# Two transformer blocks on one core: three pairs of heads kept, and a pair's solve issued later

## The chip, the cores and the metric

One core of a Trainium2 chip runs the whole program. The metric is device time in microseconds (us) of one execution; the median of three runs of the kernel before is 2461.56 us (2458.64 to 2461.78). The engines are called TensorE (PE; PEld is its weight load), VectorE (DVE), ScalarE (ACT), GpSimd (POOL) and SyncE (SP), as the profile names them.

## The reference, cut to what matters

Two blocks work on 256 tokens with 2048 channels, all in float32. The first has a gated delta rule over 16 heads of 128 channels, a convolution branch with a layer norm, gates and an output product; the second has latent attention and another convolution branch. The part that the change touches computes, for each head, in chunks (the kernel takes chunks of 128 tokens, the reference 64):

```
A = einsum(kb, k) * decay * strict            # kb = k * beta
T = triangular_solve(eye + A, eye)            # unit lower triangular inverse
u = T @ (v * beta);  w = T @ (kb * exp(gc))
v_new = u - w @ S;  o = q_dec @ S + qk @ v_new;  S = S * exp(g_last) + k_end^T @ v_new
```

and, for the convolution branch, `layernorm(u) = (u - mean) * rsqrt(mean((u - mean)^2) + eps) * g + b` over the 2048 channels of a token.

## The kernel before

Channels lie on the partitions and the 256 tokens on the free axis. Every weight matrix streams through the core as 128x512 tiles (SyncE loads them, 512 KB in one DMA). ScalarE makes a rounded copy `hi` of each (line 231), VectorE the rest `lo` (line 234), and TensorE forms each product from three matmuls (`mm3`, lines 256 to 258). `hi` and `lo` are made three to four tiles ahead of their use.

The order of all work is written out by hand: every engine executes its instructions in the order in which the program issues them. The main stream issues one `mm3` after the other; after each one `tick` (line 191) counts one tick, and then steps the background chains that are due. A chain is a generator: `yield n` puts its next step n ticks later. So a chain's delays set only where its instructions stand between those of the main stream on each engine's queue; if their data are not ready there, the engine stands still, with everything that is queued behind. `force` steps the earliest chain ahead of its time.

In the head stage each head takes 64 ticks (`group`: 16 k-tiles of four output tiles). After it the chain `evac` (line 573) convolves q, k and v into the tile `qkv`; 30 ticks after the second head of a pair has ended, the chain `delta` (line 592) of that pair begins. At most two deltas are active, so with 128 ticks for a pair the end of one overlaps with the start of the next. `head` waits at line 568 until the output of the pair that used the same `qkv` tile is done (two tiles: `heads < h - 2`). After the eight pairs come the four groups of `ga` (256 ticks; `L824` evacuates them with a sigmoid, the first at tick 64 after the last head), and later `z_b`, beside which the layer norm's chain runs.

The steps of `delta` and `output`, in ticks after the delta's first step (k, q and v of the next pair begin 128 ticks later):

```
  0  L607 eight transposes to t1 (TensorE); L614 four squares (ScalarE)
  2  L618 four squares, L619 two copies (ScalarE)
  7  L621 (VectorE), L623 pow (GpSimd)
 11  L629 to L634 coefficients (VectorE); L640 eight products (TensorE)
 15  L646 nt, 18 L646 pt (VectorE)
 20  L660 transposes, L662 (ScalarE), L668;  21 L672 (VectorE)
 25  L676 DMA dd<-dg (issued by ScalarE);  33 L678 DMA bl<-dd (ScalarE), L680 (GpSimd)
 42  L684, L686: 15 columns, two GpSimd instructions each
 84  L694 tt (VectorE)
 88  L702 transposes (TensorE), L703 copy to ta (ScalarE);  92 product, z;  96 product, L715
100  L702, L703;  104 L724;  108 L731;  112 L702, L703 copy to tt
116  L740 products, L741 copy to z;  120 L745 products, L746 copy
124  values(0): L752, L754, L759;  128 L763, L765 copy to st;  131 L769, L770, L772, L776
135  values(1);  139 L708, L781, L782
143  L793 squares;  148 L797, L799 pow (GpSimd);  152 L802;  159 L806 transposes, L808;  163 L811
```

All these chains take their PSUM banks in turn from four (`pss`). The layer norm (line 868) subtracts the mean from eight pairs of channel tiles, squares each on ScalarE and adds the squares on GpSimd (`pool_square`, seven ticks a pair); then it waits six ticks (line 888) and `rms` adds the two halves (line 324), sums over the partitions (line 330), takes the power on GpSimd (line 335) and spreads it (line 339).

Of the kernel before, what the change touches and what calls it, by code (L numbers as in the profile page):

```python
# [18 lines left out]
T = 256  # L19
# [28 lines left out]
def _mats():  # L48
# [5 lines left out]
    def put(name, v):  # L54
# [23 lines left out]
AHEAD = 3  # L78
RM = (3, 6)
WARM = 10  # L80
Y = dict(silu=8, ssq=5, pow=4, coef=2, gram=4, diag=4, dma1=8, dma2=9, rec=3, wait=21, base=4, copy=4, pred=4, vn=4, st=3, vs=4, on=3, so=5,
         f=4, scale=7)
PN = 4
RATES = (0.31, 0.10, 0.37)
# [23 lines left out]
class Build:  # L108
# [52 lines left out]
        self.idle(WARM)  # L161

    def idle(self, n):
        """Products on constants that keep the array's clock up while it waits for data."""
        if n:
            q = self.ps()
        for _ in range(n):
            self.nc.tensor.matmul(q[:, :P], self.ones, self.ones, start=True, stop=True, skip_group_check=True)
# [2 lines left out]
        self.nc.scalar.copy(hi, src)  # L171
        self.nc.vector.tensor_tensor(out=lo, in0=src, in1=hi.bitcast(F32), op=ALU.subtract)

# [1 line left out]
    def chain(self, gen, delay=0, limited=False):  # L175
        (self.waiting if limited else self.active).append([self.now + delay, gen, limited])

# [31 lines left out]
            self.step(min(self.active, key=lambda c: c[0]))  # L209
            self.admit(True)  # L210

# [1 line left out]
    def fetch(self, upto):  # L213
        while self.loaded <= min(upto, self.nhalf - 1):
            raw = self.rawp.tile([P, 2, 512], F32, tag="raw", name="raw")
# [43 lines left out]
        self.tick()  # L259

    def group(self, xs, nk=NT, done=None):
        """Four output tiles; with done, they end one after the other, and done(pb, ct) follows each."""
        pb = self.banks()

        def unit(ws, k, ct):
            s = slice(ct * P, ct * P + P)
            x = xs[ct] if isinstance(xs, list) else xs
            while x.ready <= k:
                self.force()
            self.mm3(pb[ct // 2][:, ct % 2], (ws[0][:, s], ws[1][:, s]), (x.hi[:, k], x.lo[:, k]),  # L270
                     k == 0 and ct % 2 == 0, k == nk - 1)

        for k in range(nk - 4 if done else nk):
            ws = self.kt()
            for ct in range(4):
                unit(ws, k, ct)
        if done:
            ws = self.quad()
            for n, ct in enumerate((0, 2, 1, 3)):
                for k in range(4):  # L280
                    unit(ws[k], nk - 4 + k, ct)
                done(pb, ct, n)
        return pb
# [4 lines left out]
        self.tick()  # L288

    def rows(self, xs):  # L290
        """512 outputs with the tokens on the partitions, one bank for each half of the tokens."""
        pb = self.banks()
        for k in range(NT):
            ws = self.kt()
            while xs.ready <= k:
                self.force()
            for c in range(2):
                self.unit(pb, c, xs, k, ws)
        return pb
# [7 lines left out]
            self.mm3(pb[:, 0], (hi[:, s], lo[:, s]), (xs.hi[:, k], xs.lo[:, k]), k == 0, k == NT - 1)  # L307
        return pb

# [1 line left out]
    def square_into(self, acc, src, first):  # L311
        nc = self.nc
        n = src.shape[1]
# [41 lines left out]
        return Operand(self.big(t1, F32R, name=name + "h"), self.big(t2, F32R, name=name + "l"), ready)  # L355

    def split_chain(self, make, src, x, ks, gap):
        """make(k) emits src(k); the two parts of x follow one and two steps behind."""
        nc = self.nc
        n = len(ks)  # L360
        for j in range(n + 2):
            if j < n:
                make(ks[j])
            if 1 <= j <= n:
                k = ks[j - 1]
                nc.scalar.copy(x.hi[:, k], src(k))
            if j >= 2:
                k = ks[j - 2]
                nc.vector.tensor_tensor(out=x.lo[:, k], in0=src(k), in1=x.hi[:, k].bitcast(F32), op=ALU.subtract)  # L369
                x.ready = (k.stop if isinstance(k, slice) else k + 1)  # L370
            yield gap(j)
# [4 lines left out]
        return t  # L376

    def scaled(self, src, gname, x, gap, hook):
        """x = src * g in two parts, which follow hook(k) at once and one step behind."""
        nc = self.nc  # L380
        for j in range(NT + 1):
            if j < NT:
                hook(j)
                nc.scalar.activation(x.hi[:, j], src[:, j], AF.Copy, scale=self.vec(gname, j))
            for k in ([0] if j == 0 else [j - 1] if j > 1 else []):
                nc.vector.scalar_tensor_tensor(out=x.lo[:, k], in0=src[:, k], scalar=self.vec(gname, k),
                                               in1=x.hi[:, k].bitcast(F32), op0=ALU.mult, op1=ALU.subtract)
                x.ready = k + 1
            yield gap(j)
# [39 lines left out]
            next(gen)  # L429
        self.chain(gen, delay)  # L430

# [1 line left out]
    def glu(self, j, xs, scaled=False):  # L433
        nc = self.nc
        pb = self.group(xs)
# [126 lines left out]
    def head(self, wk, h):  # L562
        nc = self.nc
        tl = lambda name, shape, **k: wk.tile([P] + shape, F32, tag=name, name=name, **k)
        pb = self.group(self.h)
        a = h % 2
        if a == 0:
            while self.heads < h - 2:
                self.force()
            self.pair = (tl("qkv", [2, 3, T], bufs=2), tl("zs", [2, T], bufs=3))  # L570
        qkv, zs = self.pair

        def evac():
            src = (pb[0][:, 0], pb[0][:, 1], pb[1][:, 0])
            w = lambda i, j: self.vec("w_qkv", (i * H + h) * 4 + j)
            for i in range(3):
                nc.scalar.activation(qkv[:, a, i], src[i], AF.Copy, scale=w(i, 3))
            nc.scalar.activation(zs[:, a], pb[1][:, 1], AF.Silu)
            yield 2
            for s in range(1, 4):  # L580
                for i in range(3):
                    nc.vector.scalar_tensor_tensor(out=qkv[:, a, i, s:], in0=src[i][:, :T - s], scalar=w(i, 3 - s),
                                                   in1=qkv[:, a, i, s:], op0=ALU.mult, op1=ALU.add)
                    yield 2
            nc.scalar.activation(qkv[:, a], qkv[:, a], AF.Silu)
            yield Y["silu"]
            if a:
                self.chain(self.delta(wk, h - 1, qkv, zs), 0, True)

        self.chain(evac())  # L590

    def delta(self, wk, h, qkv, zs):
        """Two heads, h and h + 1; four chunks f = 2 a + c of 128 tokens."""
        nc = self.nc
        mm = nc.tensor.matmul
        kw = dict(start=True, stop=True, skip_group_check=True)
        tl = lambda name, shape, **k: wk.tile([P] + shape, F32, tag=name, name=name, **k)
        half = lambda c: slice(c * P, c * P + P)
        ident = self.mat("ident")
        AC = [(a, c) for a in range(2) for c in range(2)]  # L600
        four = lambda t: t.rearrange("p (f t) -> p f t", f=4)
# [14 lines left out]
        for a in range(2):  # L616
            for j in (0, 1):
# [6 lines left out]
                                op=ALU.pow)  # L624
        yield Y["pow"]
        nk, nb = tl("nk", [2, 2]), tl("nb", [2, 2])
# [8 lines left out]
        vs = qkv[:, :, 2].rearrange("p a (c t) -> p a c t", c=2)  # L635
        gr = []
        for a in range(2):
            g = self.ps()
# [22 lines left out]
        for a, c in AC:  # L661
            nc.scalar.activation(vs[:, a, c], t2[:, half(2 * a + c)], AF.Copy, scale=nk[:, a, c:c + 1])  # L662

        # inverses of the diagonal blocks of 16, one column after the other
        b16 = self.blk[:, 0:P]
        bl = tl("bl", [16, 4, 16])
        flat = bl.rearrange("p l c i -> p (l c i)")
# [25 lines left out]
        z, vn = tl("z", [4, P]), tl("vn", [2, 2, P])  # L693
# [70 lines left out]
        st = tl("st", [2, P])  # L764
# [9 lines left out]
        on = nt.rearrange("p (a c) t -> p a c t", a=2)  # L774
# [93 lines left out]
    def layernorm(self):  # L868
        nc = self.nc
        cv = self.cv  # L870
        acc = self.new_acc()
        nc.gpsimd.tensor_tensor(out=acc, in0=cv[:, 0:2], in1=cv[:, 2:4], op=ALU.add)
        for c in range(2, 8):
            nc.gpsimd.tensor_tensor(out=acc, in0=acc, in1=cv[:, 2 * c:2 * c + 2], op=ALU.add)
        yield 32
        q = self.ps()
        for a in range(2):
            nc.tensor.matmul(q[:, :T], self.ones, acc[:, a], start=(a == 0), stop=(a == 1))
        mb = self.nrm.tile([P, T], F32, tag="rb", name="rb", bufs=3)
        nc.scalar.activation(mb, q[:, :T], AF.Copy, scale=1.0 / D)  # L880
        yield 4
        sq = self.new_acc()
        for c in range(8):
            s = slice(2 * c, 2 * c + 2)
            nc.vector.tensor_tensor(out=cv[:, s], in0=cv[:, s], in1=self.bc(mb, 2), op=ALU.subtract)
            self.pool_square(sq, cv[:, s], c == 0)
            yield 7
        yield 6
        got = []
        yield from self.rms(sq, D, got)  # L890
        yield 3
        for c in range(8):
            s = slice(2 * c, 2 * c + 2)
            nc.vector.tensor_tensor(out=cv[:, s], in0=cv[:, s], in1=self.bc(got[0][1], 2), op=ALU.mult)
            yield 3
            for k in (2 * c, 2 * c + 1):
                nc.scalar.activation(cv[:, k], cv[:, k], AF.Silu, scale=self.vec("ln_g", k), bias=self.vec("ln_b", k))
# [502 lines left out]
        self.final(mx, x)  # L1400

    def final(self, xs, x):
        """w_out_2 with tokens on the partitions; x goes there by the array's transposes."""
        nc = self.nc
        wk = self.ctx.enter_context(self.tc.tile_pool(name="fin", bufs=1))
        g = wk.tile([P, D], F32, name="g_row")
# [41 lines left out]
        for j in range(3):  # L1448
            pb = self.rows(xs)
# [3 lines left out]
        pb = self.banks()  # L1453
# [119 lines left out]
```

## Time and profile before

| what | value |
|---|---|
| median of three runs | 2461.56 us |
| span of the profiled execution (the page shows no time of its own beside it) | 2464.7 us |
| TensorE busy | 2399.9 us (97%) |
| TensorE weight loads busy | 2279.6 us (92%) |
| VectorE busy | 1655.2 us (67%) |
| ScalarE busy | 1321.8 us (54%) |
| GpSimd busy | 182.1 us (7%) |
| weights read by SyncE's queue | 417.99 MB |
| head stage | about 255 to 735 us of the span |
| layer norm's sum of squares | about 990 to 1020 us |

The profile is of one execution. Times are counted from the start of the span. A line such as `L702` names the source line that issued the instruction; `s` is a PSUM bank of the background chains, `pb` one of the main stream. The granted clock is a share of TensorE's full 2.4 GHz: 1.00, or 0.50 for its lower level, 1.2 GHz. All DMAs are issued by SyncE and ScalarE.

### The profile page before, as it was taken

To read this page: it belongs to the slowest core of one execution; us is meant where nothing else is said; L and a number is where in the kernel's file an instruction comes from. 1 tells how busy PE (TensorE), PEld (TensorE's weight loads), DVE (VectorE), ACT (ScalarE), POOL (GpSimd) and SP (SyncE) were. 2 spreads that over 40 slices of the span, in tenths; PEclk is the share of its full clock that TensorE was granted. 3 is DMA by queue.
4 is the path that set the end of the run, shared out by engine and by line. 5 is a ranking of instruction groups with operands and counts; after the bars stand their busy time and mean duration, and the time that the engine had idled before them with its cause. 6 is when DMAs were issued, how large, how long until landed. Compare 5 with 4: busy or idle time off the path is not lost.

```text
span 2464.7 us, 47419 instructions
## 1 busy us (share of the span) xinstructions
PE 2399.9 (97%) x18400; PEld 2279.6 (92%) x18400; DVE 1655.2 (67%) x3103; ACT 1321.8 (54%) x2647; POOL 182.1 (7%) x318
## 2 busy tenths in 40 slices
PE   9999999999999999999999799999999999999998
PEld 8999999999999999999999798988889999998887
DVE  7987666666688988766676875565555556554655
ACT  6544465555655444654556555555445455554454
POOL 2000222222221000100010300000000000000000
PEclk9999999999999999999999999999999999999999
DMA  6565544444444655455645453435555555556654
GB/s 217 179 192 185 172 147 146 147 147 147 146 146 144 197 185 189 163 196 191 216 169 187 153 184 132 145 130 188 189 189 183 197 201 196 192 193 207 206 194 155
DMA packets 120401, 433.93 MB, mean 176 GB/s; under 512 B 14448, under 2 KB 15344, under 8 KB 119664
## 3 DMA queue, kind: packets, MB, share of 16 engines
q1 hardware_dynamic: 116496, 417.99, 50.7%
q10 hardware_dynamic: 3680, 12.92, 1.7%
q8 instruction: 144, 2.36, 0.4%
q14 instruction: 81, 0.66, 0.1%
HBM read 426.40 MB, written 4.46 MB: 175 GB/s over the span
## 4 chain that ended last, share of the span: by engine, by line
PE 84%; DMA 5%; POOL 4%; DVE 4%; issue 2%; ACT 1%; SPq 0%; DVEq 0%; POOLq 0%; ACTq 0%
PE pb L256 26%; PE pb L258 26%; PE pb L257 26%; DMA bl<-dd 3%; POOL uu L686 2%; POOL jk L684 2%; PE s L708 1%; DVE lo L234 1%; DMA dd<-dg 1%; PE s L702 1%; DMA raw<-in_w_glu 1%; PE s L640 0%; PE s L1204 0%; PE s L1205 0%; ACT hi L231 0%
## 5 line engine op out<-in xcount | busy, mean ns | idle before, releaser
L234 DVE TENSOR_TENSOR lo<-raw,hi 128x512 fp32r<-128x512 f32 x1576 | 1075.6, 699 | 469.8 <-ACT hi L231 465.3
L231 ACT CAST hi<-raw 128x512 fp32r<-128x512 f32 x1576 | 947.7, 621 | 642.0 <-PE pb L257 262.2
L256 PE MATMUL pb<-h1h,hi 128*128 128x256 f32 x2176 | 625.0, 287 | 0.0
L258 PE MATMUL pb<-h1h,lo 128*128 128x256 f32 x2176 | 611.1, 281 | 2.7 <-DVE lo L234 2.6
L257 PE MATMUL pb<-h1l,hi 128*128 128x256 f32 x2176 | 610.5, 281 | 0.0
L258 PEld LDWEIGHTS pb<-h1h,lo 128*128 128x128 f32 x2176 | 414.8, 191 | 4.1 <-DVE lo L234 4.1
L257 PEld LDWEIGHTS pb<-h1l,hi 128*128 128x128 f32 x2176 | 415.6, 191 | 0.2
L256 PEld LDWEIGHTS pb<-h1h,hi 128*128 128x128 f32 x2176 | 413.9, 190 | 2.0
L256 PE MATMUL pb<-h2h,hi 128*128 128x256 f32 x1280 | 356.4, 278 | 0.0
L257 PE MATMUL pb<-h2l,hi 128*128 128x256 f32 x1280 | 354.1, 277 | 0.0
L258 PE MATMUL pb<-h2h,lo 128*128 128x256 f32 x1280 | 354.1, 277 | 0.0
L256 PEld LDWEIGHTS pb<-h2h,hi 128*128 128x128 f32 x1280 | 240.3, 188 | 1.1 <-issue 1.0
L257 PEld LDWEIGHTS pb<-h2l,hi 128*128 128x128 f32 x1280 | 240.9, 188 | 0.1
L258 PEld LDWEIGHTS pb<-h2h,lo 128*128 128x128 f32 x1280 | 240.3, 188 | 0.0
L475 DVE SCALAR_TENSOR_TENSOR cv<-u,vecs,cv 128x256 f32<-128x256 f32 x480 | 223.6, 483 | 0.0
L258 PE MATMUL pb<-hi,h2l 128*128 128x512 f32 x256 | 101.3, 396 | 0.0
L257 PE MATMUL pb<-lo,h2h 128*128 128x512 f32 x256 | 101.0, 394 | 0.0
L256 PE MATMUL pb<-hi,h2h 128*128 128x512 f32 x256 | 100.9, 394 | 0.0
L1439 POOL TENSOR_TENSOR rf<-rf,mhalf 128x1 f32<-128x1 f32 x2 | 1.1, 550 | 1010.7 <-DVE rf L1437 1010.7
L256 PE MATMUL pb<-x1h,hi 128*128 128x256 f32 x256 | 71.8, 281 | 3.3 <-ACT e L944 3.3
L257 PE MATMUL pb<-x1l,hi 128*128 128x256 f32 x256 | 71.8, 281 | 1.6 <-DVE x1l L369 1.6
L258 PE MATMUL pb<-x1h,lo 128*128 128x256 f32 x256 | 72.0, 281 | 0.0
(377 smaller groups left out, 4287.7 us busy)
## 6 DMA issues: line engine op xcount, KB each, us to landing
raw<-in_w_head SPq DMA_DIRECT2D x128, 512.0 KB, 4.4
raw<-in_w_cv SPq DMA_DIRECT2D x128, 512.0 KB, 4.6
raw<-in_w_glu SPq DMA_DIRECT2D x63, 512.0 KB, 4.7
raw<-in_w_ga SPq DMA_DIRECT2D x32, 512.0 KB, 4.2
raw<-in_w_gb SPq DMA_DIRECT2D x32, 512.0 KB, 4.6
raw<-in_w_ya SPq DMA_DIRECT2D x32, 512.0 KB, 4.6
raw<-in_w_zb SPq DMA_DIRECT2D x32, 512.0 KB, 3.8
raw<-in_w_yb SPq DMA_DIRECT2D x32, 512.0 KB, 4.1
```

Source lines behind the costliest of these rows:

```text
L231: nc.scalar.copy(hi, self.raws[n // 2][:, n % 2])
L234: nc.vector.tensor_tensor(out=lo, in0=self.raws[m // 2][:, m % 2], in1=self.tiles[m][0].bitcast(F32), op=ALU.subtract)
L256: mm(out, a[0], b[0], start=start, stop=False, skip_group_check=True)
L257: mm(out, a[0], b[1], start=False, stop=False, skip_group_check=True)
L258: mm(out, a[1], b[0], start=False, stop=stop, skip_group_check=True)
L475: nc.vector.scalar_tensor_tensor(out=dst, in0=src, scalar=w, in1=dst, op0=ALU.mult, op1=ALU.add)
L684: nc.gpsimd.tensor_tensor(out=jk[:, :, l + 1:], in0=bl[:, l, :, l + 1:], in1=uu[:, :, l:l + 1].to_broadcast([P, 4, n]), op=ALU.mult)
L686: nc.gpsimd.tensor_tensor(out=uu[:, :, l + 1:], in0=uu[:, :, l + 1:], in1=jk[:, :, l + 1:], op=ALU.add)
L702: nc.tensor.transpose(q[:, half(f)], src[:, f], ident)
L708: mm(q[:, half(f)], x[:, f], y[:, f], **kw)
L1439: nc.gpsimd.tensor_tensor(out=t[:, 2:3], in0=t[:, 1:2], in1=self.mhalf, op=ALU.pow)
```

## The change

The `qkv` tile gets three buffers instead of two and `zs` four instead of three, and the check of line 568 looks one pair further back. Three of the delays in `delta` grow: `dma1` (between the two DMAs) from 8 to 10, `dma2` (before GpSimd's columns) from 9 to 15, `wait` (before L694) from 21 to 30. In the table of steps the DMA bl<-dd moves from 33 to 35, the columns from 42 to 50, L694 from 84 to 101, and everything behind it by 17 as well (L702 at 105, L740 at 133, L745 at 137, L793 at 160, L799 at 165, L802 at 169, L806 at 176, L811 at 180). In the layer norm the delay ahead of `rms` is 16 ticks instead of 6. The scratch memory that the program sets aside for DMA descriptors is set to 1024. Some comments go, with the line numbers unchanged.

```diff
-Y = dict(silu=8, ssq=5, pow=4, coef=2, gram=4, diag=4, dma1=8, dma2=9, rec=3, wait=21, base=4, copy=4, pred=4, vn=4, st=3, vs=4, on=3, so=5,
+Y = dict(silu=8, ssq=5, pow=4, coef=2, gram=4, diag=4, dma1=10, dma2=15, rec=3, wait=30, base=4, copy=4, pred=4, vn=4, st=3, vs=4, on=3, so=5,
...
-            while self.heads < h - 2:
+            while self.heads < h - 4:
                 self.force()
-            self.pair = (tl("qkv", [2, 3, T], bufs=2), tl("zs", [2, T], bufs=3))
+            self.pair = (tl("qkv", [2, 3, T], bufs=3), tl("zs", [2, T], bufs=4))
...
             self.pool_square(sq, cv[:, s], c == 0)
             yield 7
-        yield 6
+        yield 16
         got = []
...
-    nc = _bacc.Bacc("TRN2", target_bir_lowering=False, num_devices=1)
+    nc = _bacc.Bacc("TRN2", target_bir_lowering=False, num_devices=1, dynamic_dma_scratch_size=1024)
```

## Rows read from the trace of the kernel before

**Rows 1.** TensorE's waits: who waited for whom, us in total, times, longest
```profile
PE s L702 <- DVE tt L694: 28.0, 8, 5.0
...
PE s L330 <- DVE acc L324: 2.4, 2, 2.1
```

**Rows 2.** Timeline of TensorE: start, duration, instruction, count, [idle before <- releaser]
```profile
303.62 1.12 PE L702 MATMUL s<-mats,tt 128*128 128x128 f32 x4 [4.95 <-DVE tt L694]
...
611.24 1.09 PE L702 MATMUL s<-mats,tt 128*128 128x128 f32 x4 [3.82 <-DVE tt L694]
...
734.67 1.09 PE L702 MATMUL s<-mats,tt 128*128 128x128 f32 x4 [4.56 <-DVE tt L694]
...
780.83 0.39 PE L258 MATMUL pb<-h1h,lo 128*128 128x256 f32 x1 [1.27 <-DVE lo L234]
```

**Rows 3.** Stretches: length, busy PE, PEld, DVE, ACT, POOL, granted clock, DMA share, GB/s
```profile
302.94:306.35 3.41, 2.73 (x13) 2.73 (x14) 2.67 (x5) 1.10 (x2) 0.00 (x0) 0.50 0.14 50
...
487.26:490.67 3.41, 3.41 (x18) 3.41 (x17) 1.91 (x4) 1.10 (x2) 0.00 (x0) 0.50 0.29 108
548.70:552.11 3.41, 2.84 (x14) 2.87 (x15) 2.61 (x5) 1.10 (x2) 0.00 (x0) 0.50 0.05 18
610.14:616.96 6.82, 5.72 (x27) 5.75 (x28) 2.98 (x5) 1.43 (x3) 0.21 (x1) 0.50 0.22 77
671.00:681.00 10.00, 7.87 (x69) 7.90 (x70) 5.96 (x12) 5.03 (x11) 0.94 (x5) 1.00 0.26 82
733.02:739.84 6.82, 5.17 (x25) 5.20 (x26) 4.08 (x8) 1.10 (x2) 0.62 (x3) 0.50 0.30 108
...
778.00:1000.00 222.00, 220.73 (x1874) 220.43 (x1874) 192.16 (x373) 104.53 (x180) 10.71 (x9) 1.00 0.56 186
...
1016.09:1019.50 3.41, 3.41 (x19) 3.41 (x19) 1.32 (x3) 0.00 (x0) 1.10 (x1) 0.53 0.65 208
```

**Rows 4.** Timeline of TensorE at the full clock, one step of the main stream
```profile
1020.40 0.28 PE L256 MATMUL pb<-h1h,hi 128*128 128x256 f32 x1
...
1020.74 0.28 PE L256 MATMUL pb<-h1h,hi 128*128 128x256 f32 x1
```

**Rows 5.** Timeline of GpSimd, the columns of pair 2 and one step of pair 7
```profile
411.88 0.29 POOL L684 TENSOR_TENSOR jk<-bl,uu 128x60 f32<-128x60 f32 x1 [10.86 <-DMA bl<-dd]
...
419.07 0.60 POOL L686 TENSOR_TENSOR uu<-uu,jk 128x36 f32<-128x36 f32 x1
...
420.40 0.25 POOL L686 TENSOR_TENSOR uu<-uu,jk 128x32 f32<-128x32 f32 x1
...
424.65 0.21 POOL L686 TENSOR_TENSOR uu<-uu,jk 128x4 f32<-128x4 f32 x1
...
722.07 0.37 POOL L686 TENSOR_TENSOR uu<-uu,jk 128x56 f32<-128x56 f32 x1
```

**Rows 6.** Timeline of VectorE beside them
```profile
418.81 1.41 DVE L234 TENSOR_TENSOR lo<-raw,hi 128x512 fp32r<-128x512 f32 x2
424.89 0.69 DVE L694 TENSOR_TENSOR tt<-uu,blk 128x512 f32<-128x512 f32 x1 [4.67 <-POOL uu L686]
...
721.77 0.95 DVE L475 SCALAR_TENSOR_TENSOR cv<-u,vecs,cv 128x256 f32<-128x256 f32 x2
```

**Rows 7.** Timeline of ScalarE around the DMA bl<-dd of pairs 2 and 7
```profile
404.80 0.62 ACT L171 CAST oah<-tt 128x512 fp32r<-128x512 f32 x1 [2.07 <-DMA dd<-dg]
...
710.81 0.60 ACTq L678 DMA_DIRECT2D bl<-dd  x1
711.44 1.28 ACT L824 ACT_TABLE_LOAD   x1 [0.36 <-issue]
712.73 1.57 ACT L824 ACTIVATE ga<-pb,vecs 128x256 f32<-128x256 f32 x4
```

**Rows 8.** Timeline of ScalarE at the start of a pair's solve
```profile
326.42 0.28 ACT L614 ACTIVATE junk<-s 128x128 f32<-128x128 f32 x1
...
329.51 0.26 ACT L619 COPY kt<-s 128x128 f32<-128x128 f32 x1
```

## The prediction

> **What bounds the kernel now.** I read the page's busy table and slices first (in the profile section): TensorE is 97% busy and near full clock in most slices, so only stretches in which TensorE stands still or runs at the low clock can be won. The list of TensorE's waits comes next [rows 1]: 28.0 us in eight waits of L702 (the first transposes of a pair's inverse) for tt of L694, all in the head stage; and the wait of L330 for the layer norm's accumulator, 2.1 us. The rest of the list lies elsewhere and is not touched. Then the timeline of TensorE around these waits [rows 2] (one per pair, up to 4.95 us; four of the eight are shown), and the granted clock behind them [rows 3]: after seven of the eight waits, and after the layer norm's, the clock is 0.50, the 1.2 GHz level, for 3.41 us or twice that. Behind the wait of pair 6 it stays at 1.00, and the 1.27 us wait at 780.83 us lies in a stretch of 222 us whose clock is 1.00 throughout [rows 2, 3].
>
> What the clock costs: work done at 0.50 takes twice as long, so half of the busy time in each stretch is lost. Busy times are 2.73 (pair 0), 3.41 (pairs 1, 2 and 3, which are alike; the third is shown), 2.84 (4), 5.72 (5) and 5.17 (7): half of the sum is 13.3 us. For the layer norm it is half of 3.41, 1.7 us. In all 28.0 + 13.3 + 2.1 + 1.7 = 45.1 us hang on these two sites.
>
> **The wait, step by step.** A tick is one step of the main stream, three matmuls, 0.34 us [rows 4] (1020.40 to 1020.74; 0.342 from longer runs of them). From the DMA dd<-dg to L694 there are 59 ticks, 20.2 us. In that time dd has to land, bl has to land, and GpSimd's 30 steps (L684, L686) have to run. For pair 2 GpSimd alone goes from 411.88 to 424.86, 13.0 us [rows 5], and VectorE, which stands at L694 behind its own queue, waits 4.67 us for the last of them [rows 6].
>
> **Third buffers, heads < h - 4, the scratch size.** No instruction is added, so I cost them at nothing. No DMA is issued by GpSimd in the list of issues, so nothing uses the scratch; the smaller one makes room for the third qkv and fourth zs tile. The third qkv is needed: pair p's output ends 163 ticks after its solve begins (now) and 180 (then); the check that guards the tile comes 162 ticks after, by the table of steps and the 64 ticks of a head. With two tiles the loop would force the chains on, out of step, by 18 ticks instead of one; with three the check looks one pair, 128 ticks, further back.
>
> **dma1 8 to 10.** The issue of bl<-dd sits in ScalarE's queue and waits there for dd; the cast behind it waited 2.07 us for dd [rows 7]. So bl starts at dd's landing, not at the tick, and two ticks later costs the solve nothing. Bounds: 0 to 2 x 0.34 = 0.7 us per pair, hidden by the 17 ticks below; I take 0, as that row has it.
>
> **dma2 9 to 15, wait 21 to 30.** They put L694 and all behind it 17 ticks, 5.8 us, later in every queue (15 of them from these two). GpSimd starts as before, when bl lands; its pow for the earlier pair's output (L799) is now issued at tick 165 and the recursion behind it at 178, so it is not caught behind the DMA wait. Of the six middle pairs the largest wait is 3.82 (pair 5, [rows 2]), so the delay covers them if GpSimd gets no slower by 2 us.
>
> Here is the one thing that the change itself slows. A GpSimd step takes 0.60 us beside VectorE's lo subtraction (L234) and 0.25 while VectorE stands idle [rows 5, 6]; the second 15 of the 30 steps now run in VectorE's idle time (420.40 to 424.86, 0.30 each, against 0.57 each from 411.88 to 420.40). Once L694 comes later, VectorE has lo work there: 17 ticks hold 4.25 of them (one every four ticks), each stretching one step by 0.35: 1.5 us. Bounds: 0, and 15 x (0.57 - 0.30) = 4.0 us; I take 1.5, since the small steps keep the rate of the idle time between two lo. Then pairs 1 to 6 keep nothing (3.82 + 1.5 - 5.8 < 0), and pair 0 keeps 4.95 + 1.5 - 5.8 = 0.6 us, too short to lower the clock by the row at 780.83.
> The Trainium skill (SBUF — State Buffer, Who interferes with whom) says that a VectorE instruction with two SBUF inputs and a GpSimd one that reads SBUF shut each other out for a whole instruction. The lo rows agree; beside the conv step L475, which has two such inputs as well, a GpSimd step took 0.37 [rows 5, 6], so here the trace does not. By the rule in full the upper bound, 4.0, would be the value; that is the second rival.
>
> **Pair 7.** Its bl is issued at tick 35 instead of 33 of its solve. The gate's evacuation L824 with its table load stands at tick 34: 711.44 to 714.30, just behind the bl issue at 710.81 now [rows 7], and ahead of it then. Added to it are the four squares of pair 6's output (1.6 us, by the four of L614 and the same again, [rows 8]) and a cast of 0.6: bl starts some 5 us later, and 4.56 + 5 + 1.5 - 5.8 = 5.3. I let this pair keep what it has, 4.6 of wait and 2.6 of clock. Bounds: none to 8 us.
>
> **What is late next.** A pair's last 31 ticks (14 now) lie beside the first 31 of the next. ScalarE's burst of eight squares and two copies (L614 to L619) lasts from 326.42 to 329.77, 3.35 us [rows 8]. Now it falls behind the copy st; then it will stand between the copies L703, L741 and the products L745, which come nine ticks after the burst begins. Counting on from L607: transposes 0.5, burst with L703 in it 0.5 to 4.4, a cast to 5.0, L741 to 5.4; TensorE gets to L745 at nine ticks plus what it does of both solves, 4.9. So L745 waits 0.5 us, with all main matmuls behind it, and the casts behind L741 have 16 ticks to spare. Later, at ticks 32 to 48 of the next pair's solve, L793, bl, L577, L578 and L802 queue on ScalarE ahead of the transposes L806; the same count gives 0.6 us. No wait of this kind is in the trace; bounds per pair are 0 and one whole burst each, 3.35; I take the counts. Seven overlaps: 7 x 1.1 = 7.7 us. At 0.5 or 0.6 the clock stays up (row at 780.83).
>
> **Layer norm, 6 to 16.** L324 and L330 come 10 ticks, 3.4 us, later, more than the 2.1 us wait; the chain behind shifts by 10 of 256 ticks, and its last two tiles wait for the z_b groups in either case. Gain 2.1 + 1.7 = 3.8; bounds 0 and 3.8. If L339 were then late it would cost up to 1 us; at full clock its six ticks come after GpSimd's pow.
>
> **Sum.** Waits 28.0 - 0.6 - 4.6 = 22.8; clock 13.3 - 2.6 = 10.7; layer norm 3.8; new waits -7.7. That is 29.6 us off. The profiled execution has its span, 2464.7, and the page shows nothing around it: 2435.1. The median of the runs shown is 3.1 us below that span, so 2432.
>
> **Rivals.**
> (1) No new wait, and pair 7 covered too: all 45.1 go, 2416.5. For it: ScalarE is 54% busy. Against: the counts above.
> (2) The wait only shrinks. With 4.0 instead of 1.5, pairs 1 to 6 keep 18.5 (28.0 less pairs 0 and 7) - 6 x 1.8 = 7.7 us, two of them about 2 us and with a low clock (3.4); pair 0 keeps 3.2 with 1.4 of clock: 15.1 more than forecast, 2447. For it: the 0.57 per step while VectorE was full. Against: it was full because of a head's evacuation just before.
> (3) Slower: the burst on ScalarE decides. If in each overlap TensorE waits a whole burst, 3.35, and the clock then stays low as behind pair 5, 2.86, seven overlaps cost 43.4 against 37.3 won elsewhere: 2468. It wins from 5.3 us per overlap. Against: L741's own data come early, and products four ticks apart leave 1.4 us each.
> (4) It does not do what it says: the loops that force chains on still run (a tile freed late), the solve is issued as early as now, and only the layer norm gains: 2458 to 2462.
>
> **How the numbers follow.** Forecast 62%, alone 2422 to 2443; (1) 15%; (2) 12%; (3) 5%; (4) 6%, half of it within 0.2% (5 us, about what a measurement can tell from no change). The range 2416 to 2447 leaves out (3), (4) and the outer part of (1) and (2). Faster 0.91, same 0.04, slower 0.05.
>
> **What would show it.** L702's wait for L694 gone from TensorE's list but for pair 0 and pair 7; clock 1.00 through the head stage but at the end; new waits of about half a us at L745 and L806; L330's wait gone. Wrong if GpSimd's 30 steps take 16 us or more, if bl of pair 7 starts as early as now, or if waits at L745 are over 1.3 us and the clock falls behind them.

## The result, and the profile after

The changed kernel takes 2418.76 us (median of four runs, 2416.15 to 2426.88) against 2460.1 (2457.64 to 2461.78) for the kernel before beside it: ratio 0.9829, interval 0.981 to 0.9848. Forecast were 2432 and a range of 2416 to 2447. The profiled execution has a span of 2415.3 us (its run: 2417.21) against 2464.7, which is 49.4 us less. The medians differ by 41.3 us: the profiled execution of the kernel before is longer than each of its four timed runs, so a part of the 49.4 us is what one execution differs from another.

TensorE's waits after (who waited for whom, us in total, times, longest), answering [rows 1]:
```profile
PE s L702 <- DVE tt L694: 3.5, 6, 0.7
...
PE pb L258 <- DVE lo L234: 1.7, 3, 0.9
...
PE s L330 <- DVE acc L324: 0.3, 1, 0.3
```
24.5 of the 28.0 us at L702 are gone. No wait at L745 or L806 is in TensorE's list. The timeline of TensorE (start, duration, instruction, count, [idle before <- releaser]) shows what is left of pair 0 and pair 7, and the longest wait of the stage, answering [rows 2]:
```profile
304.50 0.66 PE L702 MATMUL s<-mats,tt 128*128 128x128 f32 x4 [0.64 <-DVE tt L694]
...
706.01 0.66 PE L702 MATMUL s<-mats,tt 128*128 128x128 f32 x4 [0.56 <-DVE tt L694]
...
749.03 0.38 PE L258 MATMUL pb<-h1h,lo 128*128 128x256 f32 x1 [0.90 <-DVE lo L234]
```
Stretches with their granted clock, columns as in [rows 3], around those two places and over the whole head stage:
```profile
705.00:708.00 3.00, 2.44 (x21) 2.24 (x21) 2.74 (x6) 1.13 (x3) 0.21 (x1) 1.00 0.68 213
748.00:751.00 3.00, 2.10 (x19) 1.97 (x18) 3.00 (x6) 1.12 (x2) 0.43 (x1) 1.00 0.25 56
...
255.00:760.00 505.00, 500.51 (x4488) 490.84 (x4487) 379.04 (x811) 314.17 (x818) 123.04 (x268) 1.00 0.51 158
```
The same 505 us of the kernel before:
```profile
255.00:760.00 505.00, 477.03 (x4180) 468.19 (x4179) 345.07 (x748) 294.37 (x769) 109.82 (x263) 0.97 0.45 147
```
The clock is 1.00 throughout, and 4488 matmul records fit where 4180 did. So the site that the prediction named paid in full: 24.5 us of waiting and the loss at the 1.2 GHz level behind it, and at the layer norm 2.1 us of waiting and the loss behind that. The prediction priced the two losses at half of the busy time, 13.3 and 1.7 us. The kernel before shows a little less, at a granted clock of 0.50:
```profile
1016.69 0.41 PE L258 MATMUL pb<-h1h,lo 128*128 128x256 f32 x1
...
1019.25 0.41 PE L258 MATMUL pb<-h1h,lo 128*128 128x256 f32 x1
```
Between these two lie four ticks, twelve main matmuls, so one follows the other after 0.2133 us; at 1.00 it is 0.1133 [rows 4]. That is 1.88 times as long, not twice, so 0.47 of the busy time is lost: 12.5 and 1.6 us, if the other products slow down alike. The two sites make 40.7 of the 49.4 us between the two spans (41.6 at the prediction's price).

**The other 8.7 us.** From 800 to 900 us both kernels run the `ga` groups; there TensorE never idles and its clock is 1.00. Before, then after (columns as above):
```profile
800.00:900.00 100.00, 100.00 (x851) 100.00 (x850) 88.53 (x182) 49.07 (x87) 1.61 (x1) 1.00 0.59 193
```
```profile
800.00:900.00 100.00, 100.00 (x884) 100.00 (x884) 90.32 (x185) 49.20 (x86) 2.91 (x2) 1.00 0.60 191
```
Busy share and clock are the same, yet 33 more matmuls run. The timeline shows how. Before, then after:
```profile
850.66 0.28 PE L256 MATMUL pb<-h1h,hi 128*128 128x256 f32 x1
850.77 0.28 PE L257 MATMUL pb<-h1l,hi 128*128 128x256 f32 x1
850.89 0.28 PE L258 MATMUL pb<-h1h,lo 128*128 128x256 f32 x1
851.01 0.28 PE L256 MATMUL pb<-h1h,hi 128*128 128x256 f32 x1
```
```profile
850.59 0.28 PE L256 MATMUL pb<-oah,hi 128*128 128x256 f32 x1
850.71 0.28 PE L257 MATMUL pb<-oal,hi 128*128 128x256 f32 x1
850.82 0.28 PE L258 MATMUL pb<-oah,lo 128*128 128x256 f32 x1
850.93 0.28 PE L256 MATMUL pb<-oah,hi 128*128 128x256 f32 x1
```
Each matmul lasts 0.28 us in both, but they start 0.1178 us apart on average before and 0.1133 after (100 us by 851 and by 884 records agrees: 0.1175 and 0.1131). I call these the wide and the narrow spacing. Counted over the span in runs of nine main matmuls, before has 680 us at the wide spacing and after 543. At 3.8% each (1 - 0.1133/0.1178) this costs 26.0 and 20.7 us, which explains 5.3 of the 8.7 us. No step of the prediction had it. TensorE's list of waits comes to 56.4 us before and 25.8 after; 26.6 of the difference lie at the two sites, and the other 4.0 come off as well. Against that, outside of the two sites TensorE is busy for 15.7 us at the low level after, for 12.3 before, which costs some 1.6 us more. So 1.0 us stays unassigned.

### The profile page after: what moved, and what is told of

The parts are those of the page before. It is cut to its first block, busy times and chain, and to the rows that moved or that the text cites. A ratio compares the mean times of both kernels' runs of the same rounds, so it can differ in the third digit from the quotient of the medians.

```text
span 2415.3 us, 47398 instructions
## 1 busy us (share of the span) xinstructions
PE 2381.1 (99%) x18400; PEld 2262.1 (94%) x18400; DVE 1654.4 (68%) x3103; ACT 1320.9 (55%) x2647; POOL 188.9 (8%) x318
## 4 chain that ended last, share of the span: by engine, by line
PE 84%; DVE 4%; DMA 4%; POOL 4%; issue 2%; ACT 1%; SPq 0%; DVEq 0%; POOLq 0%; ACTq 0%
PE pb L256 26%; PE pb L258 26%; PE pb L257 26%; DMA bl<-dd 3%; POOL jk L684 2%; POOL uu L686 2%; DVE lo L234 1%; PE s L708 1%; DVE t L395 1%; PE s L640 1%; PE s L702 0%; PE s L1204 0%; PE s L1205 0%; DMA raw<-in_w_lat 0%; ACT hi L231 0%
## 5 line engine op out<-in xcount | busy, mean ns | idle before, releaser
L258 PE MATMUL pb<-h1h,lo 128*128 128x256 f32 x2176 | 605.0, 278 | 1.2 <-DVE lo L234 1.2
L257 PEld LDWEIGHTS pb<-h1l,hi 128*128 128x128 f32 x2176 | 409.6, 188 | 0.2
L475 DVE SCALAR_TENSOR_TENSOR cv<-u,vecs,cv 128x256 f32<-128x256 f32 x480 | 225.3, 487 | 0.0
L582 DVE SCALAR_TENSOR_TENSOR qkv<-pb,vecs,qkv 128x255 f32<-128x255 f32 (+2 forms) x144 | 65.8, 477 | 11.6 <-ACT qkv L577 11.4
```

The source lines that it names most:

```text
L257: mm(out, a[0], b[1], start=False, stop=False, skip_group_check=True)
L258: mm(out, a[1], b[0], start=False, stop=stop, skip_group_check=True)
L475: nc.vector.scalar_tensor_tensor(out=dst, in0=src, scalar=w, in1=dst, op0=ALU.mult, op1=ALU.add)
```

## Experiments

Times are medians; each ratio is to the kernel before on the same chip, with its interval. Edits are against the changed kernel except where said.

**The old delays in the changed kernel.**
```diff
-dma1=10, dma2=15, wait=30
+dma1=8, dma2=9, wait=21
```


> The changed kernel with the three old delays (8, 9, 21); the third buffers, the looser check, the small scratch and the layer norm's 16 ticks stay. If the waits of L702 and the low clock behind them are the gain, they come back: 28 us of waits in the list, 0.50 stretches behind most, and about 2456 us (2460 less some 4 of the layer norm). If a part of the gain is due to the buffers or to where the tiles lie, the time stays under 2445.


2463.35 us (2458.55 to 2471.72), ratio 1.0025 (1.0009 to 1.004). TensorE's waits, and the clock behind the first of them:
```profile
PE s L702 <- DVE tt L694: 36.1, 8, 5.5
...
302.00:312.00 10.00, 8.38 (x56) 8.38 (x57) 4.13 (x7) 3.92 (x9) 0.63 (x3) 0.70 0.18 52
```
The wait is back, with the low clock (44.4 us of it from 255 to 1040, some 16 us lost). It is 8.1 us more than in the kernel before, and the time is 7 us above what was expected; what makes it more was not separated. Since all of the gain goes with the delays, they carry it: third buffers, scratch and the layer norm's 16 ticks give nothing without them.

**Two buffers and the old check, with the new delays.**
```diff
-            while self.heads < h - 4:
+            while self.heads < h - 2:
...
-            self.pair = (tl("qkv", [2, 3, T], bufs=3), tl("zs", [2, T], bufs=4))
+            self.pair = (tl("qkv", [2, 3, T], bufs=2), tl("zs", [2, T], bufs=3))
```


> The changed kernel with two qkv tiles, three zs tiles and the old check (heads < h - 2). The output of a pair then has 18 ticks to go at the check and is forced in one go, so TensorE should stand at L806 until ScalarE's squares, GpSimd's power and ScalarE's scaling are through: some 4.5 us and a low clock of 1.7 behind it, for six pairs, 37 us: about 2456. If the third buffer is idle capacity, the time stays at 2419.


2440.33 us (2436.02 to 2440.64), ratio 0.9924 (0.9905 to 0.9943). TensorE's waits, and the first of them on TensorE and ScalarE:
```profile
PE s L806 <- ACT nt L802: 13.5, 6, 2.2
...
336.75 1.20 PE L806 MATMUL s<-mats,nt 128*128 128x128 f32 x4 [2.25 <-ACT nt L802]
...
336.30 1.28 ACT L802 ACTIVATE nt<-nt,f 128x128 f32<-128x128 f32 x4 [1.31 <-POOL f L799]
```
The loop forces the end of the earlier pair out of step: L802 waits for GpSimd's power, and TensorE for L802. All six waits last 2.25 us, half of what was expected. Five have a low clock behind them (17.05 us, some 8 lost); behind the first, shown here, it stays at 1.00. The third buffers and the looser check are thus worth 21.6 us in the changed kernel, though they add and remove no instruction.

**All the delay in one place.** The delays add up to the same tick for L694.
```diff
-dma1=10, dma2=15, wait=30
+dma1=8, dma2=9, wait=38
```


> The changed kernel with the same 17 ticks put into one delay: dma1 8, dma2 9, wait 38. TensorE's order is the same instruction for instruction; bl is issued two ticks and GpSimd's columns eight ticks earlier in their queues. If only L694's place counts, the time is that of the changed kernel, 2417 to 2420, with L702's waits at 0 to 0.7 us. If dma1's two ticks delay bl, the waits that are left (3.5 us) go: about 2415. If the columns' earlier place holds back GpSimd's power L799, waits at L806 appear: 2425 or more.


2420.13 us (2415.81 to 2425.07), ratio 0.9839 (0.9823 to 0.9855): as the changed kernel (0.9829). L702's waits are 1.7 us in all. Where in the chain the ticks stand makes no difference that these times can tell, as long as L694 stands at the same place.

**About half of the delay.** L694 at tick 93 instead of 101.
```diff
-dma1=10, dma2=15, wait=30
+dma1=8, dma2=9, wait=30
```


> The changed kernel with dma1 8, dma2 9 and wait 30: L694 nine ticks later than before, eight earlier than in the change. If the wait is met by lateness alone, L702 waits 0.6 + 8 x 0.34 = some 3 us per pair again, 25 us, with a low clock behind most of them (10 us): about 2450. If the gain grows evenly with the ticks, 9/17 of 41 us: 2438.


2442.76 us (2438.79 to 2451.95), ratio 0.994 (0.9923 to 0.9957). TensorE's waits, and the head stage:
```profile
PE s L702 <- DVE tt L694: 10.1, 8, 2.9
PE pb L258 <- DVE lo L234: 6.1, 12, 2.8
...
255.00:760.00 505.00, 492.11 (x4327) 477.15 (x4327) 355.18 (x775) 302.73 (x800) 117.55 (x264) 1.00 0.48 152
```
Nine of the 17 ticks bring less than half of the gain. L702 waits 10.1 us in all, not the 25 of the first theory, and the clock is 1.00 although waits reach 2.9 us. Of the 6.1 us of waiting for `lo`, 2.8 are one wait at 768.9, after the last pair's solve. From the first L607 to the last TensorE takes 17.4 us longer than in the changed kernel, 11.6 of it in long gaps between the starts of its matmuls, about 3 in the spacing, the rest in many short gaps. What makes the short ones was not separated, so neither theory (2450 or 2438) is shown.

**Three ticks more.**
```diff
-wait=30
+wait=33
```


> The changed kernel with wait 33 instead of 30, so L694 one us later. If the six waits of 0.3 to 0.7 us that are left at L702 are only lateness of the solve, 3.5 us go: about 2415. If GpSimd slows down with every tick that VectorE works beside it, or if the later steps meet a new wait on ScalarE, the time stays at 2419 or rises.


2416.04 us (2415.32 to 2417.82), ratio 0.983 (0.9812 to 0.9848). L702's waits are 0.3 us in all, and nothing new comes up in TensorE's list but one wait of 0.5 at L806. GpSimd's 30 steps take 16.1 us here (mean of pairs 1 to 6) against 14.7 in the changed kernel, so they do slow down further; it stays hidden because `bl` arrives sooner (told below, with the solve). Not to be told from the changed kernel, since only 3.2 us were left there.

**The layer norm's delay, taken back, and alone.** First in the changed kernel, then (sign reversed) as the only edit of the kernel before.
```diff
-        yield 16
+        yield 6
```


> The changed kernel with the layer norm's old six ticks. If the wait of L330 and its low clock cost what the trace of before shows, 2.1 + 1.7 us come back: about 2422.5. If they were covered by something else, 2419.

> The kernel before with the layer norm's delay at 16 alone. Theory A (the wait of 2.1 us and the low clock behind it go, as the prediction's term has it): 3.8 us less, ratio 0.9985. Rival B (in the changed kernel the edit was worth nothing; the wait depends on how fast the main stream's 66 ticks before it run, and what is saved is given back in the matmuls' pace): 0 to 1 us less, ratio 0.9996 to 1.0, the wait of L330 gone from the trace all the same.


Taken back: 2416.06 us (2414.41 to 2420.49), ratio 0.9836 (0.9816 to 0.9856), so no loss is measured; but 3.8 us would be 0.0015 in the ratio, which the interval does not exclude. The wait it brings back, on TensorE:
```profile
969.11 0.61 PE L330 MATMUL s<-ones,acc 128*128 128x1 f32 x4 [0.92 <-DVE acc L324]
```
It is 0.92 us, not 2.1, with the clock at 1.00: the matmuls before it run at the wide spacing here and at the narrow one in the kernel before, so the 66 ticks of the squares take 0.9 us longer and the squares are nearly ready. Alone: 2459.22 (2453.52 to 2469.88) against 2464.9, ratio 0.9993 (0.9973 to 1.0013). Its profile has neither the wait nor the low clock there, but pair 6's L702 now has a low clock behind it, which it had not before. The interval holds both theories; open.

**The scratch, alone and in the middle.** The kernel before with 1024, then the changed kernel with 8192, a larger size that still leaves room for the third buffers.
```diff
-    nc = _bacc.Bacc("TRN2", target_bir_lowering=False, num_devices=1)
+    nc = _bacc.Bacc("TRN2", target_bir_lowering=False, num_devices=1, dynamic_dma_scratch_size=1024)
```


> The kernel before with the scratch for DMA descriptors at 1024 and nothing else; every engine's order is the same. In the kernels with the small scratch the weight queue's packets took 3 to 4% longer in total, and bl landed 1 to 2 us later after its issue. If the scratch (and with it the place of the tiles) does that, bl lands later here too, L702 waits some 8 us longer in total, and the time is about 2468. If not, 2459 and the trace of before.

> The changed kernel with the scratch at 8192 instead of 1024, nothing else. With the small scratch alone the kernel before took 2463.72 against 2457.82 us. Theory A (the small size itself makes the DMAs a little slower, and a larger one mends it): 2411 to 2415 us, ratio to before about 0.981, and the weight queue's share falls from 53-54% to about 51%. Rival B (what cost 5 us there was where the matmuls' two paces fell, not the scratch): 2415 to 2420, as the changed kernel, 0.983, the share unchanged.


Alone: 2463.72 (2457.04 to 2470.41), ratio 1.002 (1.0008 to 1.0032). With 8192: 2423.43 (2418.84 to 2426.14), ratio 0.9832 (0.9802 to 0.9863), and the weight queue's share 54.0%, not lower. The kernel before with only the layer norm's delay edited, at the size of before, has 53.0%, so the share does not follow the scratch. The 0.2% of the first run has no mechanism that these runs show; its own profile (span 2455.1) is even shorter than that of before. The run with the old delays, which has 1024 too, lies as far above the kernel before (1.0025), so a cost of some 0.2% stays possible.

**A product that might set the spacing.** One 128-column product on constants at the start of each group after the head stage.
```diff
-        pb = self.banks()
+        pb = self.banks(); self.kick and self.idle(1)    # kick: set True after the head stage
```


> The changed kernel with one 128-column product of constants at the start of each group of four output tiles after the head stage (56 products, their results not used). In the traces the main stream's matmuls follow each other at 0.1133 us in some stretches and at 0.1178 in others, all at the full clock; the stretches change where another product stands between. If such a product brings the faster pitch back, up to 15 us of the slow stretches behind the head stage go, for 3 us of products: about 2408. If the pitch is not set by this, 2420 to 2425.


2438.93 us (2435.13 to 2444.77), ratio 0.9922 (0.9908 to 0.9935): 20 us worse than the changed kernel. Wide spacing goes from 543 to 818 us of the span, 10.5 us in cost; the rest lies in the products themselves and the breaks around them, which I did not separate. So such a product does not restore the narrow spacing.

**Scratch 8192 and three ticks more.**
```diff
-wait=30 ... dynamic_dma_scratch_size=1024
+wait=33 ... dynamic_dma_scratch_size=8192
```


> The scratch at 8192 and wait at 33 (L694 three ticks later than in the changed kernel). If the last 0.6 us waits at L702 and the scratch both count: 2408 to 2413 us. If neither is more than the matmuls' pace from run to run: 2414 to 2419, not to be told from the changed kernel.


2423.1 us (2417.71 to 2424.12), ratio 0.9833 (0.9802 to 0.9863): no better than the changed kernel. No version here beats it measurably. Six kernels, whose TensorE waits come to 22.0 to 28.2 us in all, can be put in the order of what the wide spacing costs them: 16.1 us (six ticks in the layer norm; span 2414.2), 18.1 (three more ticks; 2413.2), 20.7 (changed; 2415.3), 23.8 (this one; 2420.3), 26.5 (scratch 8192; 2422.7), 27.8 (all in one place; 2421.5). But for two pairs of neighbours the spans follow it, so more of what differs among these six executions goes with the spacing than with the waits.

## Why the prediction came out as it did

The time came out inside the stated range, but 13 us below the 2432 and outside of the 2422 to 2443 that the forecast alone was given. Two terms of the sum are wrong, the new waits and pair 7, and both erred to the same side.

**Right: the place, and nearly the price.** The wait of L702, the clock behind it (12.5 us instead of 13.3), that the delay must cover it, and that the tile needs a third buffer: shown by the old delays (all back) and by two buffers (21.6 us back). The ratio fell to the faster side as forecast with 0.91.

**Wrong: the new waits, 7.7 us, did not come.** That the burst on ScalarE falls between L703, L741 and L745 is right; what failed is my count for TensorE. ScalarE and TensorE around L745 of pair 0:
```profile
317.27 0.28 ACT L614 ACTIVATE junk<-s 128x128 f32<-128x128 f32 x1 [0.51 <-PE s L607]
...
318.74 0.58 ACT L703 COPY tt<-s 128x512 f32<-128x512 f32 x1
...
321.51 0.37 ACT L741 COPY z<-s 64x256 f32<-64x256 f32 x1
```
```profile
316.64 1.03 PE L607 MATMUL s<-mats,qkv 128*128 128x128 f32 x8
...
321.97 0.68 PE L745 MATMUL s<-tt,z 64*64 64x64 f32 x8
```
ScalarE ends L741 at 321.88, 5.2 us after L607 begins, where I had 5.4. TensorE reaches L745 after 5.3, where I had 4.9: nine ticks and the work of two solves take longer in its queue than I summed. The margin is 0.09 us instead of -0.5, and 0.08 to 0.15 in all seven overlaps. That no wait came is thus luck as far as this forecast goes: a tenth of a microsecond more on ScalarE would have made one. The 0.6 us that I had at L806 for every overlap came once, for pair 6; pair 2 and pair 6:
```profile
455.45 0.60 PE L806 MATMUL s<-mats,nt 128*128 128x128 f32 x4
...
684.86 1.19 PE L806 MATMUL s<-mats,nt 128*128 128x128 f32 x4
```
For pair 6 ScalarE reaches L802 only at 684.38, behind L824 and its table load, and the four products wait 0.6 us for it in all. Longer waits came only where two buffers put L806 out of step.

**Wrong by size, without consequence: the solve** (GpSimd's 30 steps L684 and L686, for whose end L694 waits, and the two DMAs ahead of them). Compare [rows 5, 6] with GpSimd, then VectorE, for pair 2:
```profile
403.03 0.40 POOL L684 TENSOR_TENSOR jk<-bl,uu 128x60 f32<-128x60 f32 x1 [7.02 <-DMA bl<-dd]
...
413.76 0.57 POOL L686 TENSOR_TENSOR uu<-uu,jk 128x24 f32<-128x24 f32 x1
414.41 0.31 POOL L684 TENSOR_TENSOR jk<-bl,uu 128x20 f32<-128x20 f32 x1
...
417.47 0.21 POOL L686 TENSOR_TENSOR uu<-uu,jk 128x4 f32<-128x4 f32 x1
```
```profile
413.48 0.74 DVE L234 TENSOR_TENSOR lo<-raw,hi 128x512 fp32r<-128x512 f32 x1 [1.19 <-ACT hi L231]
414.15 0.47 DVE L475 SCALAR_TENSOR_TENSOR cv<-u,vecs,cv 128x256 f32<-128x256 f32 x1
...
417.71 0.69 DVE L694 TENSOR_TENSOR tt<-uu,blk 128x512 f32<-128x512 f32 x1 [2.46 <-POOL uu L686]
```
GpSimd's 30 steps take 14.7 us on the mean of pairs 1 to 6 against 13.3 before: 1.3 more, forecast 1.5. Again a step beside `lo` takes 0.57 and one beside L475 0.31. The Trainium skill (SBUF — State Buffer, Who interferes with whom), read in full, had given 4.0 here; the trace decides against that for L475. What I missed is `bl`, which I put at 0 later. On ScalarE, for pair 2 and pair 7 (answering [rows 7]; ACTq is a DMA issued from its queue):
```profile
390.00 0.32 ACTq L676 DMA_DIRECT2D dd<-dg  x1
...
394.32 0.31 ACT L793 ACTIVATE junk<-nt 128x128 f32<-128x128 f32 x1
394.46 0.60 ACTq L678 DMA_DIRECT2D bl<-dd  x1
...
680.61 1.28 ACT L824 ACT_TABLE_LOAD   x1
681.91 0.47 ACT L824 ACTIVATE ga<-pb,vecs 128x256 f32<-128x256 f32 x1
681.97 0.60 ACTq L678 DMA_DIRECT2D bl<-dd  x1
```
At tick 35 the issue stands behind the four squares L793 of the pair before, so `bl` starts 4.4 us after `dd` instead of 3.1 (pairs 1 to 6), and its data reach GpSimd 1.5 us later still. In the run with two buffers, where TensorE stands still while `bl` is under way, that last step takes 6.4 to 7.0 us instead of 8.6 to 9.6; that the weight stream beside it is the cause was only argued.

It is the squares that moved in, not the two ticks of `dma1`: with 17 ticks more they stand at tick 160 - 128 = 32 of the next pair's solve. For pair 7 the prediction counted them, for the other pairs it did not. ScalarE at pair 2 with all the delay in one place (`bl` at tick 33), then with three ticks more (the squares at tick 35, behind the issue):
```profile
392.75 0.31 ACT L793 ACTIVATE junk<-nt 128x128 f32<-128x128 f32 x1
392.81 0.60 ACTq L678 DMA_DIRECT2D bl<-dd  x1
```
```profile
391.00 0.60 ACTq L678 DMA_DIRECT2D bl<-dd  x1
...
391.64 0.31 ACT L793 ACTIVATE junk<-nt 128x128 f32<-128x128 f32 x1
```
In the first of these runs `bl` starts 4.3 us after `dd` although `dma1` is back at 8; in the second after 3.3, and its data reach GpSimd 7.7 us after that, as in the kernel before (7.8; 9.3 in the changed kernel). From `dd` to the end of the solve pairs 1 to 6 thus take some 4 us more, not 1.5.

**Why it was covered all the same.** Between the issue of `dd` and L702, TensorE now has 240 matmuls of the main stream instead of 188, and the product L708 (0.8 us), which belongs to the earlier pair and moved in with its 17 ticks. Without the wait this takes 28.8 us against 22.0: the cover grew by 6.8 us for these pairs, not 5.8. For pair 7 it grew by 8.2 (29.58 less 21.34). There `bl` came 4.1 us later behind the table load, as forecast (some 5), and `dd` to the end of the solve took 29.35 instead of 25.03, so 4.56 + 4.3 - 8.2 leaves 0.7; the row at 706.01 has 0.56. The step that failed is "I let this pair keep what it has": 6.6 us.

**The layer norm's 3.8 us** are in the spans of these two profiles, but the edit has not been shown to earn them. In the changed kernel it is worth nothing measurable.

**Sum.** To 29.6 us add 7.7 (no new waits) and 6.6 (pair 7), take off 2.3 for pairs 0 to 6 (they keep 2.9, not 0.6): 41.6, or 40.7 with the low clock at its measured price. The outcome is that of rival (1), which had 15%; I had put its chance too low, since its two conditions, margins of half a microsecond, were within the error of my counts.

## What to carry to other kernels

When an engine stands at a fixed place of a hand-written order, what counts is the sum of everything between the issue and the use on that engine's queue, other chains' work that moves in with it included, and not the delay in ticks. A buffer that removes no instruction can be the one that lets the delay work: count from allocation to release in the same ticks. A forecast wait of half a microsecond from summed durations over five microseconds is not a forecast; give it even chances.

## What the runs showed that was not expected

At a granted clock of 1.00, with no idle time, 256-column matmuls with a weight load each follow one another at 0.1133 or at 0.1178 us, for unbroken stretches of up to 348 us at the narrow and 221 us at the wide spacing. Most changes between the two lie at waits or where another product stands between, but in neither direction reliably: after 780.83 [rows 2] the kernel before is at the wide one until about 989. And they need neither: at about 1120.4 us the changed kernel goes from wide to narrow and at about 1140.5 us back, each time between two main matmuls with no wait and no other product near. What sets the spacing stays open. A 3.8% difference over 1400 us of such matmuls is as large as many edits.

Waits with a full clock behind them reach 2.9 us (half of the delay), and waits of 2.25 us with a low one behind them occur (two buffers, where one of six equal waits has the full clock behind it). The length of a wait alone did not tell which.
